# Two transformer blocks on one core: the order of the steps from an account of every engine, lent work tiles in the swiglu parts, and the keys' norm ahead of the scans

## The chip, the cores and the metric

One Trainium2 chip, one core of it. The time is the device time of one execution of the whole program in microseconds. Below, PE is TensorE, DVE is VectorE, ACT is ScalarE, POOL is GpSimd and SP is SyncE, whose queue carries the DMA transfers.

## What is computed

Two blocks in fp32 over 256 rows of width 1024. The first block has two layers, each with a swiglu, a mixing part (RWKV-7 beside a causal attention), cross-attention to a memory of 256 rows, and a second swiglu; a final norm ends it. The second block has an adaptive norm from a condition vector, an mLSTM beside a differential attention, and a hierarchical mixture of 32 experts. Cut to what bears on the change:

```python
def first_block(x, mem, rel_bias, ...):
    for l in range(DEPTH):
        x = x + FFN_RES_WEIGHT * swiglu_ffn(rms_norm(x, ffn1_norm_g[l]), ffn1_w_in[l], ffn1_w_out[l])
        proj = rms_norm(x, mix_norm_g[l]) @ w_mix_in[l]
        y_rwkv = rwkv7_time_mix(proj[..., :RWKV_PROJ], ...)
        y_moba = moba_attention(q_m, k_m, v_m, rel_bias)
        x = x + jnp.concatenate([y_rwkv, y_moba], axis=-1) @ w_mix_out[l]
        x = x + memory_cross_attention(...)
        x = x + FFN_RES_WEIGHT * swiglu_ffn(rms_norm(x, ffn2_norm_g[l]), ffn2_w_in[l], ffn2_w_out[l])
    return rms_norm(x, final_norm_g)

def rwkv7_time_mix(p, ...):
    ...
    decay = jnp.exp(-jnp.exp(w_log))
    a = jax.nn.sigmoid(a0 + a_lo @ a_up)
    kk = k * k_k
    kk = kk / jnp.maximum(jnp.sqrt(jnp.sum(kk * kk, axis=-1, keepdims=True)), 1e-12)
    b = kk * a
    # state = state * decay + (state @ -kk) b + v k, row after row
```

## The kernel before

**Weights.** All weights lie in one array of units; half a unit is a tile of 128 by 1024 floats, 512 KB, which SP loads into `raw` (four buffers, `RING`). Since products are exact to fp32 only in parts, each tile is split: ACT copies it to a rounded form `wh` (L369), DVE subtracts that to get the rest `wl` (L370), with two buffers of each in the first block. The activations have the same two parts, `XH` and `XL`. A product of 128 by 512 is then three matmuls, high by high, high by the weight's rest, and the rest by high (L398, L399, L400). A swiglu part takes 66 such tiles. A tile of a projection feeds 12 matmuls.

**Order.** Every part of the program is a generator. It issues some instructions and then yields two numbers: how long TensorE will be at work on them, and how many microseconds must pass until its next step should be issued. `Weave.step` (L260) keeps one clock `now`, adds the first number, and sets the task's due time by the second; of the tasks that are due it takes the one of the highest priority (the lowest number). All numbers are written by hand. The program thus sets the order of each engine's queue; every engine takes its queue in order, and waits on semaphores for data or for a buffer to come free.

```python
        if callable(r):
            t.need = r
        else:
            self.now += r[0]
            t.ready = self.now + r[1]
```

**PSUM.** Eight banks: four called `acc`, two `mm` for projections, two `tr` for transposes and small sums.

**Swiglu** (`ffn`, L625). Eleven chunks of 256 columns: a projection of gate and up into `mm`, tanh on ACT and two products on DVE, four transposes (L666) into `tr`, and the product with the next weights into the four `acc` banks. Behind the last chunk the four `acc` banks are finished one after the other, DVE adds each to x (L680), and `prep` (L518) makes the next part's input: for each half of x, transposes of two tiles of rows (L534), a scaling by DVE (L540), and the split by ACT and DVE (L542, L543). While it loads weights of the swiglu, the program also folds the tiles of the condition's projection into sums on DVE (`ada`, L1349).

**Mix** (`mix`, L685). Thirteen projections run as the main task at priority 10. Beside them run tasks for RWKV: `shifted` (L726) transposes and shifts a projection's result, `rwkv_early` (L774) prepares decay, keys and receptance for one of two groups of heads (a pair of 128-wide blocks each), `rwkv_chunk` (L986) solves two chunks of 128 rows by a chain of small matmuls and copies, and `rwkv_late` (L859) applies the state and norms the result. `moba` (L1159) does the attention, `xattn_k` the keys of the cross-attention.

In `rwkv_early` the order of the text is the order in each queue: two small matmuls per block (L790, L791), then on ACT per block a tanh, two exponentials (L794 to L796) and the square of the keys (L797), on DVE two scans (L804) and two products (L806, L807), and only then the norm of the keys. The squares are summed over each head by matmuls with a matrix of ones (L813), DVE takes a maximum (L815), POOL the power −1/2 over four columns (L816), ACT spreads the result over the heads (L818), once for each half of the rows, and PE transposes it (L825). The second and the third yield between them carry guessed delays of 0.6 and 1.5 us.

**Names.** In a row `tr<-csts,t1k` is a transpose or small sum into a `tr` bank, `mm<-wh,XH` a product of a projection, `acc<-wh,X` one of a swiglu's second product. `L398` and the like are lines of the kernel.

Of the kernel before, what the change touches and what calls it, by code (L numbers as in the profile page):

```python
# [19 lines left out]
P = 128  # L20
D = 1024
KT = 8
# [214 lines left out]
class Task:  # L237


    def __init__(self, gen, prio):  # L240
        self.gen, self.prio, self.ready, self.need, self.done, self.out = gen, prio, 0.0, None, False, None
# [4 lines left out]

class Weave:


    def __init__(self):  # L250
        self.now, self.tasks = 0.0, []
# [8 lines left out]
    def step(self, top=99):  # L260
        able = []
        for t in self.tasks:
            if t.prio > top:
                continue
            if t.need is not None:
                if not t.need():
                    continue
                t.need, t.ready = None, max(t.ready, self.now)
            able.append(t)
        t = next((t for t in able if t.ready <= self.now + 1e-6), None)  # L270
        if t is None:
            t = min(able, key=lambda z: z.ready)
            self.now = t.ready
        try:
# [4 lines left out]
            return  # L279
# [22 lines left out]
class Prog:  # L302
    def __init__(self, ctx, tc, a):
        self.tc, self.nc, self.a = tc, tc.nc, a
# [9 lines left out]
        self.weave = Weave()  # L314
# [5 lines left out]
        self.behind, self.stop = [], None  # L320

# [4 lines left out]
    def ps(self, tag):  # L326
        return self.pp.tile([P, 512], F32, name=self.nm(tag), tag=tag, bufs={"acc": 4, "mm": 2, "tr": 2}[tag])
# [7 lines left out]
    def k(self, tag, n, dt=F32):  # L335

        return self.kp.tile([P, n], dt, name=self.nm(tag), tag=tag, bufs=self.bufs[tag])

    def wtile(self, tag, dt):

        n = RING[tag]
        turn = self.turn.setdefault(tag, collections.deque())
        if not turn:
            turn.extend([self.wp] * n + [self.kp] * self.bufs.get(tag, 0))
            turn.extend([self.sp] * self.spare.get(tag, 0))
        pool = turn.popleft()
        bufs = {id(self.wp): n, id(self.kp): self.bufs.get(tag, 0), id(self.sp): self.spare.get(tag, 0)}[id(pool)]
        return pool.tile([P, 1024], dt, name=self.nm(tag), tag=tag, bufs=bufs)

    def lookahead(self, tag):  # L350

        return RING[tag] + self.spare.get(tag, 0) + self.bufs.get(tag, 0)

    def raw(self, name, j, i):
# [3 lines left out]
        else:  # L358
            src = self.a["w"][UNITS[name] + j, i]
        self.nc.sync.dma_start(t, src)  # L360
        return t


    def parts(self, raw):
        h, l = self.wtile("wh", F32R), self.wtile("wl", F32R)
        with ExitStack() as later:
            for z in self.behind:
                later.enter_context(self.tc.issue_after(z.ins))
            self.nc.scalar.activation(h, raw, AF.Copy)  # L369
            self.nc.vector.tensor_sub(l, raw, h.bitcast(F32))  # L370
        return h, l

    def weights(self, name, j, i):

        self.prefetch()
# [1848 lines left out]
```

## Time and profile before

| what | value |
|---|---|
| median of 3 runs | 2004.87 us |
| lowest and highest | 2003.45 us, 2007.29 us |
| the profiled execution | 2002.69 us |
| its span | 2000.9 us |
| its mean granted clock of TensorE | 0.988 |
| TensorE busy | 1915.2 us (96%) |
| VectorE busy | 1401.1 us (70%) |
| ScalarE busy | 1064.5 us (53%) |
| moved from HBM | 378.03 MB |

The span is that of the first to the last instruction; the time of the execution has 1.8 us more around it. A busy share tells how much of the span an engine spent in instructions. A stretch in which TensorE is granted half of its clock counts as busy too. A granted clock of 1.00 is 2.4 GHz, the lower level is 1.2 GHz. In a timeline the bracket behind a row gives how long the engine stood idle before it, and what ended the idle time.

### The profile page before, as it was taken

The numbers are of one execution on the slowest core, as the hardware profiler recorded it, in microseconds if no ns is written. First come the engines' busy times: TensorE is split into PE (matmuls) and PEld (weight loads), VectorE is DVE, ScalarE is ACT, GpSimd is POOL, SyncE is SP. The second block draws the span as 40 slices with busy tenths as digits, with TensorE's granted clock in tenths as the row PEclk, the third lists the DMA queues.
The fourth block names the chain that finished last, engine by engine and source line by source line (L and its number), as shares of the span: only waits on it lengthen the run. The fifth ranks groups of instructions, "written<-read, shape, count | busy, mean of one in ns | idle before, by whom it ended". The sixth has DMA issues, their size and how long they took to land.

```text
span 2000.9 us, 26350 instructions
## 1 busy us (share of the span) xinstructions
PE 1915.2 (96%) x9572; PEld 1540.8 (77%) x9572; DVE 1401.1 (70%) x2279; ACT 1064.5 (53%) x1608; POOL 70.4 (4%) x71
## 2 busy tenths in 40 slices
PE   8999989999999999999999999999989999999998
PEld 6788768778787878787777777787768777777776
DVE  6566686765566676666767654666687767999997
ACT  4444553555544454445545555444465556777675
POOL 0000011000000000000010000000010000000000
PEclk9999989999999999999999999999989998999999
DMA  6766431344366656665323253566654344999996
GB/s 218 251 227 215 154 124 55 102 127 169 119 218 219 208 193 212 221 210 180 133 81 106 69 180 116 197 209 213 216 180 146 128 158 141 322 344 357 327 345 235
DMA packets 114807, 381.42 MB, mean 191 GB/s; under 512 B 17080, under 2 KB 21864, under 8 KB 114544
## 3 DMA queue, kind: packets, MB, share of 16 engines
q1 hardware_dynamic: 114672, 379.68, 56.2%
q8 instruction: 77, 1.26, 0.3%
q14 instruction: 58, 0.48, 0.1%
HBM read 378.03 MB, written 3.17 MB: 191 GB/s over the span
## 4 chain that ended last, share of the span: by engine, by line
PE 69%; issue 12%; DVE 10%; ACT 4%; DMA 3%; POOL 1%; SPq 0%; DVEq 0%; POOLq 0%; ACTq 0%
PE mm L398 14%; PE mm L399 14%; PE mm L400 14%; DVE wl L370 5%; PE acc L400 4%; PE acc L398 4%; PE acc L399 4%; DMA raw<-in_w_dram 3%; ACT wh L369 3%; PE acc L1060 1%; PE acc L1291 1%; PE acc L1273 1%; PE acc L1195 1%; POOL rs L504 1%; PE tr L534 1%
## 5 line engine op out<-in xcount | busy, mean ns | idle before, releaser
L370 DVE TENSOR_TENSOR wl<-raw,wh 128x1024 fp32r<-128x1024 f32 x648 | 788.6, 1227 | 370.1 <-ACT wh L369 365.8
L369 ACT ACTIVATE wh<-raw 128x1024 fp32r<-128x1024 f32 x648 | 676.6, 1057 | 566.0 <-PE mm L400 381.1
L398 PE MATMUL mm<-wh,XH 128*128 128x512 f32 (+1 forms) x1744 | 695.2, 402 | 9.6 <-ACT s L733 3.6
L399 PE MATMUL mm<-wl,XH 128*128 128x512 f32 (+1 forms) x1744 | 690.8, 396 | 10.1 <-DVE wl L370 9.8
L400 PE MATMUL mm<-wh,XL 128*128 128x512 f32 (+1 forms) x1744 | 685.0, 394 | 1.4 <-DVE XL L543 1.1
L398 PEld LDWEIGHTS mm<-wh,XH 128*128 128x128 f32 x1744 | 330.8, 190 | 89.4 <-issue 12.7
L399 PEld LDWEIGHTS mm<-wl,XH 128*128 128x128 f32 x1744 | 330.7, 190 | 84.2 <-DVE wl L370 22.0
L400 PEld LDWEIGHTS mm<-wh,XL 128*128 128x128 f32 x1744 | 330.5, 190 | 68.8 <-DVE XL L543 3.1
L398 PE MATMUL acc<-wh,X 128*128 128x512 f32 x352 | 141.9, 409 | 2.1 <-ACT wh L369 2.1
L399 PE MATMUL acc<-wl,X 128*128 128x512 f32 x352 | 140.1, 398 | 0.4 <-DVE wl L370 0.4
L400 PE MATMUL acc<-wh,T 128*128 128x512 f32 x352 | 139.3, 396 | 0.0
L399 PEld LDWEIGHTS acc<-wl,X 128*128 128x128 f32 x352 | 66.9, 190 | 15.8 <-DVE wl L370 2.2
L398 PEld LDWEIGHTS acc<-wh,X 128*128 128x128 f32 x352 | 66.2, 189 | 16.6 <-ACT wh L369 3.1
L400 PEld LDWEIGHTS acc<-wh,T 128*128 128x128 f32 x352 | 66.7, 189 | 15.5
L1349 DVE SCALAR_TENSOR_TENSOR el<-raw,vecs,el 128x512 f32<-128x512 f32 x84 | 63.1, 752 | 21.1 <-DMA raw<-in_w_dram 18.7
L653 ACT ACTIVATE t1k<-mm,rh 128x256 f32<-128x256 f32 x88 | 41.8, 475 | 58.9 <-PE mm L400 58.9
L400 PE MATMUL acc<-wh,ah 128*128 128x512 f32 x128 | 50.0, 398 | 1.2 <-DVE ah L407 1.2
L399 PE MATMUL acc<-wl,ah 128*128 128x512 f32 x128 | 50.6, 398 | 0.0
L398 PE MATMUL acc<-wh,ah 128*128 128x512 f32 x128 | 45.6, 397 | 1.4 <-ACT ah L405 1.4
L657 DVE SCALAR_TENSOR_TENSOR t1k<-mm,rh,t1k 128x256 f32<-128x256 f32 x88 | 42.6, 484 | 3.0
L655 DVE SCALAR_TENSOR_TENSOR t1k<-t1k,mm 128x256 f32<-128x256 f32 x88 | 36.8, 418 | 9.0 <-ACT t1k L653 7.3
L556 POOL TENSOR_TENSOR rs<-s,emh 128x2 f32<-128x2 f32 x11 | 8.0, 729 | 945.3 <-DVE s L554 945.3
(480 smaller groups left out, 1888.1 us busy)
## 6 DMA issues: line engine op xcount, KB each, us to landing
raw<-in_w_dram SPq DMA_DIRECT2D x696, 512.0 KB
ext<-ext SPq DMA_DIRECT2D x1, 2048.0 KB
bi<-ext SPq DMA_DIRECT2D x8, 256.0 KB
K<-in_mem_dram SPq DMA_DIRECT2D x8, 256.0 KB
x<-in_x_dram SPq DMA_DIRECT2D x4, 256.0 KB
bi<-ext SPq DMA_DIRECT2D x8, 128.0 KB
w<-gates SPq DMA_DIRECT2D x2, 512.0 KB
out_dram<-x SPq DMA_DIRECT2D x4, 256.0 KB
```

The source lines that it names most:

```text
L369: self.nc.scalar.activation(h, raw, AF.Copy)
L370: self.nc.vector.tensor_sub(l, raw, h.bitcast(F32))
L398: mm(out, xh, wh, start=start, stop=False)
L399: mm(out, xh, wl, start=False, stop=False)
L400: mm(out, xl, wh, start=False, stop=stop)
L504: nc.gpsimd.tensor_tensor(r, ms, self.emh[:, :n], op=OP.pow)
L534: nc.tensor.transpose(tp[:, j * P:(j + 1) * P], xs[t][:, j * P:(j + 1) * P], self.ident)
L653: nc.scalar.activation(th, gu[t][:, :256], AF.Tanh, scale=rh[:, t:t + 1])
L655: nc.vector.scalar_tensor_tensor(tt, th, 1.0, gu[t][:, :256], op0=OP.add, op1=OP.mult)
L657: nc.vector.scalar_tensor_tensor(h, gu[t][:, 256:], r2h[:, t:t + 1], tt, op0=OP.mult, op1=OP.mult)
L1060: mm(zp[:, bs(j)], y[:, bs(j)], RH[:, j], start=True, stop=True)
L1349: self.nc.vector.scalar_tensor_tensor(self.mod, z, c, self.mod, op0=OP.mult, op1=OP.add)
```

## The change

**Order.** A class `Clock` keeps an account: for each engine the time at which it will be free, for each tile when its parts will be written and when it was last used, for each ring of buffers when the oldest comes free. `note` is called behind every instruction (a wrapper around the engines, line L378 in the trace afterwards) and adds a duration from a formula. A step now ends with `due(tiles)`, the time at which the account has these tiles written, or `room(ring)`, when a bank comes free; or with a small number against the end of the task's last work off TensorE. `now` follows the account's TensorE. Delays of 10 and more stay as they were. Some steps are cut finer: the two softmax halves go together in three phases, the norm after the time mix yields before each transpose, a projection yields before it takes banks and before each weight tile. `moba`'s priority goes from 4 to 1.5.

**Lent tiles.** In the swiglu parts the buffers of tags `sm`, `gr` and `pt`, which only other parts use, serve as one more `raw`, `wh` and `wl` (`raw` not in the last swiglu). At a swiglu's end the last tile but one is taken with a look-ahead of one.

**Keys' norm.** In `rwkv_early` the squares and the sums come first; one maximum and one power over eight columns serve both halves of the rows; the copies stand behind the tanh and the exponentials of both blocks. All other instructions are the same in kind and number: 4 fewer on DVE and 4 fewer on POOL.

```diff
+class Clock:
+    HOP, LAP = 0.06, dict(PE=0.0, DVE=0.08, ACT=0.1, POOL=0.0)
+    ...
+    def due(self, *aps):
+        t = 0.0
+        for z in aps:
+            name, runs, *_ = self.span(z)
+            for there, end, _ in self.wrote.get(name, ()):
+                if end > t and any(a < d and c < b for a, b in there for c, d in runs):
+                    t = end
+        return At(t + self.HOP)
+
+    def room(self, ring, n):
+        held = self.rings.get(ring, ())
+        return At(self.used.get(held[0], 0.0) + self.HOP if len(held) >= n else 0.0)
...
 class Weave:
...
-        else:
-            self.now += r[0]
-            t.ready = self.now + r[1]
+        elif r is not None:
+            if isinstance(r[1], At):
+                t.ready = max(self.now, r[1])
+            elif r[1] >= 10:
+                t.ready = self.now + r[1]
+            else:
+                t.ready = max(self.now, t.end + min(r[1], 0)) if r[1] else self.now
...
     def lookahead(self, tag):
-        return RING[tag] + self.spare.get(tag, 0) + self.bufs.get(tag, 0)
+        return RING[tag] + self.spare.get(tag, 0) + self.bufs.get(tag, 0) + len(self.loan.get(tag, ()))
...
     def proj(self, X, name, j, width=512, last=0):
+        yield 0, self.room("mm")
         out = [self.ps("mm") for _ in range(2)]
...
                 wh, wl = self.weights(name, j + u, i)
+                yield 0, self.due(wh)
...
-        w = [self.weights(name, 3 * NCH - 1, k) for k in range(2)]
+        w = [self.weights(name, 3 * NCH - 1, k, (99, 1)[k]) for k in range(2)]
...
-        C.append(self.spawn(self.moba(q, k, v, Y, [mq, mk]), 4))
+        C.append(self.spawn(self.moba(q, k, v, Y, [mq, mk]), 1.5))
...
     def rwkv_early(self, l, g, lo, rT, kT, need):
-        d, rd, sq = (self.k("el", 512) for _ in range(3))
+        sq, d, rd = (self.k("el", 512) for _ in range(3))
+        for b in range(2):
+            act(B(sq, b), B(kT, b), AF.Square, scale=vec("kk", b))
+        yield 0, self.due(sq)
+        s = self.ps("tr")
+        nr = []
+        for t in range(2):
+            for b in range(2):
+                mm(s[:, 4 * t + 2 * b:4 * t + 2 * b + 2], sq[:, b * S + t * P:b * S + (t + 1) * P], self.cst("bones"),
+                   start=True, stop=True)
+        n = self.k("s8", 8)
+        nc.vector.tensor_scalar_max(n, s[:, :8], 1e-24)
+        nc.gpsimd.tensor_tensor(n, n, self.emh[:, :8], op=OP.pow)
         zw, za = self.ps("tr"), self.ps("acc")
...
             act(B(rd, b), th, AF.Exp, bias=self.cdec[:, 1:2], scale=-DEC)
-            act(B(sq, b), B(kT, b), AF.Square, scale=vec("kk", b))
-        yield 1.0, 0
+        for t in range(2):
+            nr.append(self.k("t1k", 256))
+            nc.scalar.copy(nr[t].rearrange("p (h d) -> p h d", d=64), n[:, 4 * t:4 * t + 4, None].to_broadcast([P, 4, 64]))
+        yield 1.2, self.due(d, rd)
...
-        nr = []
-        for t in range(2):
-            s = self.ps("tr")
-            for b in range(2):
-                mm(s[:, 2 * b:2 * b + 2], sq[:, b * S + t * P:b * S + (t + 1) * P], self.cst("bones"), start=True, stop=True)
-            n = self.k("s8", 8)
-            nc.vector.tensor_scalar_max(n[:, :4], s[:, :4], 1e-24)
-            nc.gpsimd.tensor_tensor(n[:, :4], n[:, :4], self.emh[:, :4], op=OP.pow)
-            nr.append(self.k("t1k", 256))
-            nc.scalar.copy(nr[t].rearrange("p (h d) -> p h d", d=64), n[:, :4, None].to_broadcast([P, 4, 64]))
-        yield 0.1, 0.6
-        yield 0, 1.5
+        yield 0, self.due(*nr)
...
+LOAN = dict(raw=["sm"], wh=["gr"], wl=["pt"])
...
+                    p.lend({k: v for k, v in LOAN.items() if n < 7 or k != "raw"})
                     yield from p.ffn(f"ffn{part // 2 + 1}{l}", X)
+                    p.lend({})
```

On PE, at the keys' norm of the second pair of blocks in layer 0, before (`tr<-csts,el` are the sums of L813, `tr<-csts,t1k` the transposes of L825, `mm` the large products):

```order
L398 MATMUL mm_2351<-wh_2430,XH_1749 128x512
L399 MATMUL mm_2351<-wl_2431,XH_1749 128x512
L400 MATMUL mm_2351<-wh_2430,XL_1750 128x512
L813 MATMUL tr_2475<-csts,el_2442 128x2
L813 MATMUL tr_2483<-csts,el_2442 128x2
L813 MATMUL tr_2475<-csts,el_2442 128x2
L813 MATMUL tr_2483<-csts,el_2442 128x2
L825 MATMUL tr_2524<-csts,t1k_2481 128x128
L825 MATMUL tr_2552<-csts,t1k_2481 128x128
L825 MATMUL tr_2524<-csts,t1k_2489 128x128
L825 MATMUL tr_2552<-csts,t1k_2489 128x128
L398 MATMUL mm_2538<-wh_2499,XH_1749 128x512
```

The same place on PE in the changed kernel (`acc<-lora,waup` and `tr<-lora,waup` are the small matmuls of L791 and L790):

```order
L378 MATMUL mm_2363<-wh_2366,XL_1745 128x512
L378 MATMUL tr_2441<-csts,el_2436 128x2
L378 MATMUL acc_2450<-lora_1778,waup_1869 128x256
L378 MATMUL tr_2441<-csts,el_2436 128x2 x3
L378 MATMUL mm_2362<-wh_2414,XH_1744 128x512
L378 MATMUL mm_2362<-wl_2415,XH_1744 128x512
L378 MATMUL tr_2449<-lora_1778,waup_1869 128x256 x2
L378 MATMUL mm_2362<-wh_2414,XL_1745 128x512
```

Sums and transposes stood back to back; now 30 large products stand between them, 28 of them behind the last small matmul. For the first pair 10 stood between the first sums and the transposes, and 5 between the last sums and these; now 13 do.

On PE at the end of the first swiglu, before (`acc` are its last products, `tr<-csts,x` the transposes of L534; `x_72` and `x_73` are the two row tiles, each named once for either half of its columns):

```order
L398 MATMUL acc_106<-wh_1711,X_1687 128x512
L399 MATMUL acc_106<-wl_1712,X_1687 128x512
L400 MATMUL acc_106<-wh_1711,T_372_1688 128x512
L534 MATMUL tr_1752<-csts,x_72 128x128 x4
L534 MATMUL tr_1766<-csts,x_73 128x128 x4
L534 MATMUL tr_1797<-csts,x_72 128x128 x4
L534 MATMUL tr_1818<-csts,x_73 128x128 x4
L398 MATMUL mm_1764<-wh_1717,XH_1749 128x256
```

The same place in the changed kernel:

```order
L378 MATMUL acc_104<-wh_1701,T_376_1696 128x512
L378 MATMUL tr_1747<-csts,x_72 128x128 x4
L378 MATMUL tr_1756<-csts,x_73 128x128 x4
L378 MATMUL acc_106<-wh_1674,X_1695 128x512
L378 MATMUL acc_106<-wl_1675,X_1695 128x512
L378 MATMUL acc_106<-wh_1674,T_376_1696 128x512
L378 MATMUL acc_106<-wh_1701,X_1695 128x512
L378 MATMUL acc_106<-wl_1702,X_1695 128x512
L378 MATMUL acc_106<-wh_1701,T_376_1696 128x512
L378 MATMUL tr_1809<-csts,x_72 128x128 x3
L378 MATMUL mm_1779<-wh_1719,XH_1744 128x256
```

The first half's eight transposes moved ahead of the last six products; those of the second half now alternate with the first products of the next part.

On PE at the start of the first two chunks in layer 0, before (`tr<-csts,Y`, `acc<-X,A`, `acc<-Y,T` and `acc<-RH,Y` are steps of the chain of `rwkv_chunk`, once for each chunk):

```order
L1040 MATMUL tr_2624<-csts,Y_2233 128x128 x4
L398 MATMUL mm_2538<-wh_2590,XH_1749 128x512
L1040 MATMUL tr_2631<-csts,Y_2265 128x128 x4
L399 MATMUL mm_2538<-wl_2591,XH_1749 128x512
L400 MATMUL mm_2538<-wh_2590,XL_1750 128x512
L1046 MATMUL acc_2651<-X_2629,A_2234 128x128 x4
L1046 MATMUL acc_2659<-X_2636,A_2266 128x128 x4
L1053 MATMUL acc_2667<-Y_2233,T_609_2656 128x128 x4
L1053 MATMUL acc_2673<-Y_2265,T_611_2664 128x128 x4
L399 MATMUL mm_2539<-wl_2591,XH_1749 128x512
L400 MATMUL mm_2539<-wh_2590,XL_1750 128x512
```

The same place in the changed kernel:

```order
L378 MATMUL mm_2599<-wh_2602,XH_1744 128x512
L378 MATMUL tr_2546<-csts,Y_2211 128x128 x4
L378 MATMUL tr_2553<-csts,Y_2243 128x128 x4
L378 MATMUL acc_2566<-X_2551,A_2212 128x128 x4
L378 MATMUL acc_2574<-X_2558,A_2244 128x128 x4
L378 MATMUL acc_2582<-Y_2211,T_588_2571 128x128 x4
L378 MATMUL acc_2588<-Y_2243,T_590_2579 128x128 x4
L378 MATMUL tr_2622<-csts,s_593_2594 128x128
```

The projection's products between the steps are gone; eight transposes of the attention's queries and one large product follow, and then the next steps of the chain.

## Rows read from the trace of the kernel before

**Rows 1.** Page, part 1: busy us (share of the span) xinstructions

```profile
PE 1915.2 (96%) x9572; PEld 1540.8 (77%) x9572; DVE 1401.1 (70%) x2279; ACT 1064.5 (53%) x1608; POOL 70.4 (4%) x71
```

**Rows 2.** Windows by stage: from:to length, busy by engine, clock, DMA share, GB/s

```profile
core 0: us, PE busy (x) PEld busy (x) DVE busy (x) ACT busy (x) POOL busy (x), PEclk, DMA share, GB/s
212.60:451.00 238.40, 222.78 (x1431) 178.86 (x1430) 165.59 (x368) 128.99 (x256) 22.64 (x24) 0.98 0.34 108
...
734.10:930.70 196.60, 192.85 (x878) 156.80 (x876) 130.75 (x164) 89.37 (x112) 0.70 (x1) 1.00 0.63 209
...
1452.90:1676.00 223.10, 210.98 (x1044) 168.63 (x1045) 168.44 (x348) 124.31 (x199) 19.62 (x12) 0.98 0.50 167
```

**Rows 3.** Windows around the keys' norm, layer 0 twice and layer 1 twice

```profile
247.00:258.00 11.00, 7.84 (x30) 5.67 (x30) 8.69 (x22) 5.21 (x11) 3.79 (x4) 0.84 0.30 95
286.00:298.00 12.00, 7.76 (x26) 5.66 (x26) 11.51 (x35) 6.29 (x14) 5.08 (x4) 0.72 0.23 65
966.00:974.00 8.00, 4.83 (x16) 3.19 (x15) 7.82 (x16) 4.62 (x9) 2.24 (x3) 0.79 0.42 133
1004.00:1016.00 12.00, 8.01 (x30) 5.93 (x30) 11.05 (x35) 6.69 (x15) 5.35 (x4) 0.72 0.26 67
```

**Rows 4.** Timeline, first pair, layer 0: start, us, engine, line, operation [idle before]

```profile
249.78 0.41 ACT L818 COPY t1k<-s 128x256 f32<-128x256 f32 x1 [1.08 <-POOL s L816]
...
250.24 0.44 PE L825 MATMUL tr<-csts,t1k 128*128 128x128 f32 x2 [1.05 <-ACT t1k L818]
...
252.50 0.50 PE L398 MATMUL mm<-wh,XH 128*128 128x512 f32 x1 [1.82 <-ACT s L733]
```

**Rows 5.** Timeline, second pair, layer 0

```profile
286.77 0.50 ACT L796 ACTIVATE el<-t1k,cdec 128x256 f32<-128x256 f32 x1
...
288.76 0.14 DVE L815 TENSOR_SCALAR s<-tr 128x4 f32<-128x4 f32 x1
...
288.97 2.61 POOL L816 TENSOR_TENSOR s<-s,emh 128x4 f32<-128x4 f32 x2 [25.32 <-DVE s L815]
...
290.47 0.44 PE L825 MATMUL tr<-csts,t1k 128*128 128x128 f32 x2 [2.14 <-ACT t1k L818]
```

**Rows 6.** Timeline of POOL in the second block: a power over 8 columns

```profile
1530.35 1.67 POOL L504 TENSOR_TENSOR rs<-s,emh 128x8 f32<-128x8 f32 x1 [58.54 <-DVE s L502]
```

**Rows 7.** Timeline of PE in the first layer's second swiglu

```profile
606.22 0.39 PE L398 MATMUL mm<-wh,XH 128*128 128x512 f32 x1
...
606.45 0.39 PE L399 MATMUL mm<-wl,XH 128*128 128x512 f32 x1
```

**Rows 8.** Waits of PE in the first and last swiglu: us, times, longest

```profile
PE mm L399 <- DVE wl L370: 2.0, 3, 1.1
PE mm L399 <- DVE wl L370: 1.8, 4, 0.5
```

**Rows 9.** Page, part 5: xcount, busy, mean ns, idle before and releaser

```profile
L370 DVE TENSOR_TENSOR wl<-raw,wh 128x1024 fp32r<-128x1024 f32 x648 | 788.6, 1227 | 370.1 <-ACT wh L369 365.8
```

**Rows 10.** Timeline of SP near the start

```profile
48.83 0.60 SPq L485 DMA_DIRECT2D ext<-ext  x1
```

**Rows 11.** Windows near the start

```profile
58.00:62.00 4.00, 2.18 (x12) 1.58 (x10) 0.43 (x1) 0.87 (x1) 0.00 (x0) 1.00 0.92 364
62.00:66.00 4.00, 3.76 (x10) 2.95 (x11) 2.96 (x3) 1.62 (x3) 0.00 (x0) 0.57 0.46 161
```

**Rows 12.** Waits of PE over the whole span: us in total, times, longest

```profile
PE tr L534 <- DVE s L540: 4.9, 3, 1.6
...
PE tr L939 <- DVE YL L936: 2.6, 4, 0.8
...
PE tr L666 <- DVE t1k L657: 2.0, 3, 0.7
PE tr L1609 <- DVE E L1605: 1.9, 2, 1.2
```

**Rows 13.** Timeline of DVE at the end of the first swiglu

```profile
211.91 0.69 DVE L680 SCALAR_TENSOR_TENSOR x<-acc,x 128x512 f32<-128x512 f32 x1 [0.67 <-PE acc L400]
```

**Rows 14.** Windows: a chunk chain and attention in layer 0's mix

```profile
371.00:400.00 29.00, 28.99 (x273) 25.33 (x272) 16.16 (x30) 13.10 (x32) 1.19 (x2) 1.00 0.24 69
```

More of the change, by code (lines that the diff above doesn't have):

```diff
@@ new lines, with __init__, __getattr__, call @@
+class Timed:
+    def __init__(self, nc, clock):
+        self.nc = nc
+        for k, e in Clock.ENGINES.items():
+            setattr(self, k, TimedEngine(getattr(nc, k), e, clock))
+    def __getattr__(self, k):
+        return getattr(self.nc, k)
+class TimedEngine:
+    def __init__(self, eng, name, clock):
+        self.eng, self.name, self.clock = eng, name, clock
+    def __getattr__(self, op):
+        f = getattr(self.eng, op)
+        def call(*args, **kw):
+            r = f(*args, **kw)
+            self.clock.note(self.name, op, args, kw)
+            return r
+        return call
@@ L247, with __init__ @@
 class Weave:
-    def __init__(self):
-        self.now, self.tasks = 0.0, []
+    def __init__(self, clock):
+        self.now, self.tasks, self.clock = 0.0, [], clock
+        self.end = 0.0
     def add(self, gen, prio):
@@ L267, in step @@
                     continue
-                t.need, t.ready = None, max(t.ready, self.now)
+                t.need, t.ready, t.end = None, max(t.ready, self.now), max(t.end, self.end)
             able.append(t)
@@ L273, in step @@
             self.now = t.ready
+        self.clock.last = 0.0
         try:
@@ L278, in step @@
             self.tasks.remove(t)
-            return
+            r = None
+        t.end = self.end = max(t.end, self.clock.last)
+        self.now = max(self.now, self.clock.at["PE"])
         if callable(r):
             t.need = r
-        else:
-            self.now += r[0]
-            t.ready = self.now + r[1]
+        elif r is not None:
[3 more added lines that the diff above has]
+                t.ready = self.now + r[1]
+            else:
+                t.ready = max(self.now, t.end + min(r[1], 0)) if r[1] else self.now
     def finish(self, *tasks):
@@ L303, in __init__ @@
     def __init__(self, ctx, tc, a):
-        self.tc, self.nc, self.a = tc, tc.nc, a
+        self.clock = Clock()
+        self.tc, self.nc, self.a = tc, Timed(tc.nc, self.clock), a
         nc = self.nc
@@ L326, in ps, with room, due, tile @@
     def ps(self, tag):
[L327 removed]
+        n = BANKS[tag]
+        return self.tile(self.pp, [P, 512], F32, tag, tag, n)
+    def room(self, tag):
+        return self.clock.room((id(self.pp), tag), BANKS[tag])
+    def due(self, *aps):
+        return self.clock.due(*aps)
+    def tile(self, pool, shape, dt, nm, tag, n):
+        name = self.nm(nm)
+        self.clock.tile((id(pool), tag), n, name)
+        return pool.tile(shape, dt, name=name, tag=tag, bufs=n)
     @contextmanager
@@ L548, in prep @@
                     nc.scalar.activation(junk, xs[t], AF.Square, scale=D ** -0.5, accum_out=ss[:, 2 * hf + t:2 * hf + t + 1])
-            yield 0, 1.2
+                self.clock.quiet = False
+            half = slice(4 * hf, 4 * hf + 4)
+            yield 0, self.due(pair.H[:, half], pair.L[:, half])
             pair.ok[hf] = True
@@ L936, in rwkv_late @@
             tt(h4(yl), h4(yl), ss[t][:, :4, None].to_broadcast([P, 4, 64]), op=OP.mult)
+        for t in range(2):
+            yl = YL[t]
+            yield 0, self.due(yl)
             tp = self.ps("tr")
@@ L1175, in moba @@
                 nc.vector.tensor_tensor(cut[t](s), sp[:, :2 * n], cut[t](bi), op=OP.add)
-                yield 0.43 * (t + 1), 0.5
+                yield 0.43 * (t + 1), 0 if t == 0 else -0.5
             if i < 3:
                 bi = bias(*each[i + 1])
-            pv = [self.softmax(cut[t](s), cut[t](s), 2, (t + 1) * P) for t in range(2)]
-            yield 0, 4.5
+            pv = yield from self.softmax(*[(cut[t](s), cut[t](s), 2, (t + 1) * P) for t in range(2)])
             for t in range(2):
@@ L1274, in xattend @@
                                      KT[i][:, kb * S:(kb + 1) * S], start=kb == 0, stop=kb == 1)
+            sps.append(sp)
             yield 1.7, 0
-            pv.append(self.softmax(sm[:, t * 512:(t + 1) * 512], sp, 2, S))
-        yield 0, 3.5
+        pv = yield from self.softmax(*[(sm[:, t * 512:(t + 1) * 512], sps[t], 2, S) for t in range(2)])
         for i in range(2):
@@ L1318, in final_norm @@
             yield lambda: self.version[hf] >= use
-            yield 0, 0.9
+            yield 0, self.due(*[z[hf] for z in self.halves(self.x)])
             squares(0, hf)
```

254 lines of the change are left out of this document (176 added, 78 removed).

## The prediction

> **What bounds the kernel now.** I read the busy shares first, then the span cut into stages, then the stretches and the timeline around the longest stalls, then the list of TensorE's waits. The shares say that TensorE works 1915.2 of 2000.9 us, so 85.7 us are left in which it does nothing; VectorE is next with 1401.1 us [rows 1]. The time is TensorE's work plus its stalls, and the change leaves TensorE the same matmuls and transposes. So the question is only how many of the stalls go, and whether new ones come.
>
> The stages say where the stalls are [rows 2]: a swiglu part idles 196.60 − 192.85 = 3.8 us, a mix part 238.40 − 222.78 = 15.6 us, the stretch from the final norm through the second block's attention 12.1 us. The mix parts come first. Their granted clock of 0.98, against 1.00, points to a second loss, which busy time does not show: stretches in which TensorE counts as busy and runs at the lower of its two levels, 1.2 GHz.
>
> Inside a mix part both losses stand at the keys' norm [rows 3], once for each pair of head blocks. In layer 0 the first pair idles 11.00 − 7.84 = 3.2 us, and a mean clock of 0.84 over 11 us means 1.8 us of full speed lost; the second idles 4.2 and loses 12 × 0.28 = 3.4. The two places of layer 1 idle 3.2 and 4.0 us and lose 1.7 and 3.4. Together 14.6 us of idle and 10.3 us of clock, **24.9 us**.
>
> The timeline says why. The small power on GpSimd is followed by a copy on ScalarE for each half of the rows, and the transposes of L825 stand on TensorE's queue close behind. In the first pair they wait 1.05 us for the second copy, and the next product waits 1.82 us more for a copy that stood behind these on ScalarE [rows 4]. In the second pair nothing stands on TensorE between the sums of L813 and the transposes, which wait 2.14 us for the first of two powers that take 2.61 us together [rows 5].
>
> **The change part by part.**
>
> *Keys' norm first.* The squares and sums now precede the tanh, the exponentials and the scans, and one power over 8 columns takes the place of two over 4. Such a power took 1.67 us elsewhere [rows 6], against 2.61 for two [rows 5]. In the order, 13 large products now stand between sums and transposes for the first pair and 28 for the second. A large product starts 0.23 us after the one before [rows 7], so these cover 3.0 and 6.4 us. What has to fit is a maximum (0.14), the power (1.67) and two copies of 0.41: 2.6 us. For the second pair it is hidden whole. For the first it is not certain: ScalarE has six activations of 0.5 us, the tanh and exponentials, in its queue ahead of the copies [rows 5], so 3.0 + 0.8 = 3.8 us against 3.0. I leave 1 us there, with the clock staying up, and 1.3 us per layer for what ScalarE and VectorE do late: 4.6 us stay. Term **−20**; bounds −25 (all hidden) and −10 (the copies come late and the clock still falls once per layer).
>
> *Lent tiles.* The swiglu parts get a third pair of split tiles and a fifth raw tile from buffers that idle there. TensorE waits for the low half of a weight 13 times in the four parts, 6.7 us in all; the first part and the last are shown [rows 8]. Splitting a tile costs VectorE 1.23 us [rows 9], and its 12 products run 2.75 us [rows 7], so a split is late only when other VectorE work comes between. A third tile adds 2.75 us of cover to waits whose longest in these parts is 1.1 us. Term **−6**; bounds 0 (VectorE's own order is the cause) and −6.7.
>
> *Start of the program.* The 2 MB copy that spreads the bias table is issued at 48.83 us, among the weights [rows 10]. Later TensorE idles 1.8 and 0.2 us and runs 4 us at 0.57 [rows 11], 2.0 + 1.7 = 3.7 us. A fifth raw tile, and a copy issued three weight tiles earlier, cover a part: **−2**; bounds 0 and −3.7.
>
> *End of the swiglu.* The transposes of both halves of x stand together, and the later ones wait for VectorE to empty a bank: 4.9 us in three places [rows 12]. Now the first half goes ahead of the last six products (1.4 us), the second between products of the next part. What cannot be covered there is the last addition to x, 0.69 us [rows 13]. Term **−3.4**; bounds 0 and −4.9.
>
> *Guessed delays.* Of the waits behind a guess I count the three largest kinds that are left: the time mix's output transposes (2.6 us), the first chunk of a swiglu (2.0), the second block's weights E (1.9) [rows 12], 6.5 us. Where a chain is longer than the work at hand no order hides it, so I take two thirds, **−4.3**; bounds 0 and −6.5. Besides, a mix part idles 15.6 us [rows 2], of which 7.4 lie at the keys' norm in layer 0; of the other 8.2, in many short waits, I take a quarter, 2 us per layer: **−4**; bounds 0 and −16.
>
> *What it costs.* In the new order the first chunks' chain of the time mix has nearly no projection between its steps. With two pairs of blocks in two layers there are four such places, the later pair's with attention between. Two chunks alternate, each covering the other's copies. A stretch of 29 us of such chain and attention work, with little projection in it, was busy 28.99 us at clock 1.00 [rows 14]. So bare chains need not stall; but where VectorE has a weight to split in between (1.23 us, [rows 9]), a step is late. One per place: **+5**; bounds 0 and +20, four of them per place.
> A rule of the Trainium skill speaks against the change here ("TensorE: Matmul & The Clock Gate", section "A second HAM failure mode: psum-queue depth-cycling"): short idle times between groups of matmuls that cycle through PSUM banks let the clock go down and up, and the throughput suffers. By it this term would be near +50 instead of +5, as under the second rival. The stretch just named cycles through banks and does not bear it out.
>
> Sum: −20 − 6 − 2 − 3.4 − 4.3 − 4 + 5 = −34.7. The profiled execution took 2002.69 us; the median of three is 2004.87, 2.2 above. So 1968 us for such an execution and, 2.2 above it, **1970 us** for a median.
>
> **Rivals.** About 0.2%, 4 us, is what a measurement of this kernel can tell from no change.
>
> *The stalls move.* The account is a model of the chip that no trace corrects while it plans; ScalarE and VectorE take their work in order, so other instructions become late. Then what stays is what buffers and the shorter power bring: −6, −2 and half the keys' norm (−10), and the chains' +5: −13, 1992 us. For it: VectorE is busy 70% of the span [rows 1]. Against it: the largest waits stand where a whole chain was issued without any cover, and there the order changes most.
>
> *The bare chains drop the clock (slower).* If each of the four places, some 29 us long, ran at the 0.57 that those 4 us at the start had [rows 11], it would lose 29 × 0.43 = 12.5 us: +50 in place of +5. With the gains of 39.7 that is +10, 2015 us. It decides from 39.7 / 4 = 9.9 us lost in each place. For it: the clock fell after each of the idle times at the keys' norm [rows 3]. Against it: it stayed at 1.00 through such a chain [rows 14]. The skill's rule named above would give this time.
>
> *More is hidden.* If the 12 us that I leave of the mix parts' short waits go too, and half of the 12.1 us idle in the second block's attention: 1970 − 18 = 1952 us.
>
> *It orders little.* The norm's gain is lost again on the first pair's late copies and on chain steps at their upper bounds: −10 − 6 + 20, and the small terms at 0, is +4, within the 4 us of before: 2001 to 2009.
>
> **How the numbers follow.** Forecast, 1958 to 1983: 0.57. The stalls move, 1983 to 2000: 0.18. More is hidden, 1943 to 1958: 0.12. Little: 0.05. Slower: 0.08. The slower end, the unchanged case and the lower half of the best one are left out of the range, 0.19 in all, and the upper edge is drawn in a little, since the second case centres on 1992: **1951 to 1997**. Faster by over 0.2%: 0.87; the same 0.05; slower 0.08.
>
> **What would show it.** Right: at the keys' norm of either layer no idle of TensorE much over 1 us and no half clock behind it; fewer than five waits for a low half in the four swiglu parts; no wait over 1 us for the normalised x at a swiglu's end; mix parts some 12 us shorter, swiglu parts 2 to 4. Wrong: new waits of TensorE inside the chunk chains, with the clock falling behind them; or the norm's transposes still waiting for the copies, with the tanh and exponentials ahead of these.

## The result and the profile after

The changed kernel takes 1979.93 us, median of 4 runs (1978.89 to 1985.92), against 2004.16 us before; the ratio is 0.9884, with a 95% interval of 0.9860 to 0.9908. That is 24 us less where 34 were forecast, inside the range. The profiled execution took 1985.92 us, the slowest of the four and 16.8 us less than the profiled one before, so its stages show less gain than the median. Its mean granted clock is 0.987; the other three had 0.990 and 0.991.

In the profile after, nearly every instruction has line L378, that of the wrapper, and is told apart by its tiles. Part 1 of the page, to be held against [rows 1]:

```profile
PE 1913.3 (96%) x9572; PEld 1551.5 (78%) x9572; DVE 1398.0 (70%) x2275; ACT 1062.2 (54%) x1608; POOL 72.7 (4%) x67
```

The span is 1984.1 us, so 1984.1 − 1913.3 = 70.8 us of TensorE's idle time are left of 85.7: 14.9 of the 16.8 us are idle time. The windows by stage, as in [rows 2]:

```profile
208.40:440.90 232.50, 220.10 (x1424) 180.66 (x1425) 163.31 (x365) 127.00 (x252) 24.67 (x22) 0.99 0.34 108
725.40:920.00 194.60, 193.12 (x878) 157.50 (x878) 129.19 (x163) 90.12 (x116) 0.69 (x1) 1.00 0.63 206
1435.40:1660.00 224.60, 210.28 (x1050) 169.71 (x1050) 168.63 (x349) 125.81 (x203) 18.55 (x12) 0.98 0.50 166
```

The swiglu part idles 1.5 us (3.8 before), the mix part 12.4 (15.6 before), the second block 14.3 (12.1 before). At the keys' norm, first and second pair of layer 0, then of layer 1, as in [rows 3]:

```profile
232.00:247.00 15.00, 13.63 (x78) 10.73 (x76) 12.40 (x29) 11.56 (x23) 2.94 (x2) 1.00 0.30 102
280.00:292.00 12.00, 8.83 (x39) 6.60 (x38) 10.12 (x26) 7.86 (x16) 1.27 (x2) 0.72 0.25 71
...
945.00:960.00 15.00, 13.50 (x77) 10.60 (x77) 12.83 (x28) 10.54 (x21) 3.90 (x2) 1.00 0.24 81
994.00:1008.00 14.00, 10.99 (x45) 8.79 (x44) 11.10 (x27) 8.19 (x16) 1.26 (x2) 0.63 0.20 59
```

The first pairs idle 1.4 and 1.5 us at full clock: of 9.9 us lost there before (idle 3.2 and 3.2, clock 1.8 and 1.7), 2.9 are left. (A wait some 7 us behind these windows has grown; it is shown with the bare chains below.) The second pairs idle 3.2 and 3.0 us, and lose 12 × 0.28 = 3.4 and 14 × 0.37 = 5.2 us of clock: 14.8 us, against 15.0 before. There the change gained next to nothing in this execution; a second profile, shown with the changed kernel's rerun below, has 13.6 us. The timeline of the second pair in layer 0 shows why, first ScalarE, then VectorE, then TensorE:

```profile
276.96 1.06 ACT L378 ACTIVATE wh<-raw 128x1024 fp32r<-128x1024 f32 x1 [4.61 <-PE mm L378]
...
279.62 1.70 ACT L378 ACTIVATE el<-t1k,cdec 128x256 f32<-128x256 f32 x4
281.22 0.70 ACT L378 COPY t1k<-s 128x256 f32<-128x256 f32 x2
...
282.54 0.70 ACT L378 ACTIVATE s<-mm,rh 128x512 f32<-128x512 f32 x1
```

```profile
283.92 1.23 DVE L378 TENSOR_TENSOR_SCAN el<-el,start 128x512 f32<-128x512 f32 x1
...
287.45 0.87 DVE L378 SCALAR_TENSOR_TENSOR el<-K,vecs,tr 128x256 f32<-128x256 f32 x2
```

```profile
281.67 0.74 PE L378 MATMUL tr<-csts,t1k 128*128 128x128 f32 x4 [0.67 <-ACT t1k L378]
283.29 0.50 PE L378 MATMUL mm<-wh,XH 128*128 128x512 f32 x1 [0.88 <-ACT s L378]
...
287.98 1.97 PE L378 MATMUL tr<-csts,Y 128*128 128x128 f32 x8 [1.63 <-DVE el L378]
```

The power on GpSimd starts at 273.05, takes 1.64 us and is done at 274.7, but ScalarE stands idle for 4.61 us before a weight's split, whose tile TensorE still holds. The tanh, the exponentials and the norm's copies are behind it in the queue, so the copies start only at 281.22, and the transposes (0.67 us) and the next product (0.88 us) wait. A third wait is new: the transposes put their results into both `tr` banks, and VectorE reads them only at 287.45, behind the scans; until then the chunk chain's next transposes have no bank (1.63 us). The row names VectorE's `el`, the reader of these banks, and not the `Y` they transpose.

### The profile page after: what moved, and what is told of

The parts are those of the page before. It is cut to its first block, busy times and chain, and to the rows that moved or that the text cites. A ratio compares the mean times of both kernels' runs of the same rounds, so it can differ in the third digit from the quotient of the medians.

```text
span 1984.1 us, 26329 instructions
## 1 busy us (share of the span) xinstructions
PE 1913.3 (96%) x9572; PEld 1551.5 (78%) x9572; DVE 1398.0 (70%) x2275; ACT 1062.2 (54%) x1608; POOL 72.7 (4%) x67
## 4 chain that ended last, share of the span: by engine, by line
PE 72%; issue 12%; DVE 10%; ACT 3%; DMA 2%; POOL 1%; SPq 0%; DVEq 0%; POOLq 0%; ACTq 0%
PE mm L378 45%; PE acc L378 22%; PE tr L378 5%; DVE wl L378 4%; ACT wh L378 2%; DVE s L378 1%; DVE el L378 1%; DMA raw<-in_w_dram 1%; POOL rs L378 1%; DMA K<-in_mem_dram 1%; DVE XL L378 1%; DVE x L378 1%; DVE AR L378 0%; DVE t1k L378 0%; ACT s L378 0%
## 5 line engine op out<-in xcount | busy, mean ns | idle before, releaser
L378 DVE TENSOR_TENSOR wl<-raw,wh 128x1024 fp32r<-128x1024 f32 x648 | 786.3, 1225 | 370.6 <-ACT wh L378 368.8
L378 ACT ACTIVATE wh<-raw 128x1024 fp32r<-128x1024 f32 x648 | 676.1, 1057 | 538.8 <-PE mm L378 368.5
L378 PE MATMUL mm<-wh,XH 128*128 128x512 f32 (+1 forms) x1744 | 698.2, 402 | 10.9 <-ACT s L378 3.3
L378 PE MATMUL mm<-wl,XH 128*128 128x512 f32 (+1 forms) x1744 | 687.4, 394 | 3.8 <-DVE wl L378 3.5
L378 PE MATMUL mm<-wh,XL 128*128 128x512 f32 (+1 forms) x1744 | 685.6, 393 | 2.7 <-DVE XL L378 2.7
L378 PEld LDWEIGHTS mm<-wh,XH 128*128 128x128 f32 x1744 | 330.3, 190 | 84.7 <-issue 8.1
L378 PEld LDWEIGHTS mm<-wl,XH 128*128 128x128 f32 x1744 | 330.1, 189 | 78.5 <-DVE wl L378 13.3
L378 PEld LDWEIGHTS mm<-wh,XL 128*128 128x128 f32 x1744 | 329.6, 189 | 74.7 <-DVE XL L378 4.0
L378 PE MATMUL acc<-wh,X 128*128 128x512 f32 x352 | 143.0, 406 | 0.0
L378 PE MATMUL acc<-wl,X 128*128 128x512 f32 x352 | 139.0, 395 | 0.0
L378 PE MATMUL acc<-wh,T 128*128 128x512 f32 x352 | 138.8, 394 | 0.0
L378 PE MATMUL acc<-wh,ah 128*128 128x512 f32 x256 | 85.9, 398 | 2.9 <-ACT ah L378 1.5
L378 DVE SCALAR_TENSOR_TENSOR el<-raw,vecs,el 128x512 f32<-128x512 f32 x84 | 63.1, 751 | 34.1 <-DMA raw<-in_w_dram 32.6
L378 PEld LDWEIGHTS acc<-wh,T 128*128 128x128 f32 x352 | 66.3, 188 | 16.1
L378 PEld LDWEIGHTS acc<-wl,X 128*128 128x128 f32 x352 | 66.4, 189 | 13.8
L378 PEld LDWEIGHTS acc<-wh,X 128*128 128x128 f32 x352 | 66.2, 188 | 13.6
L378 POOL TENSOR_TENSOR rs<-s,emh 128x2 f32<-128x2 f32 (+2 forms) x28 | 30.7, 1100 | 1195.1 <-DVE s L378 1187.8
L378 ACT ACTIVATE t1k<-mm,rh 128x256 f32<-128x256 f32 x88 | 41.8, 474 | 53.0 <-PE mm L378 52.6
L378 PEld LDWEIGHTS acc<-wh,ah 128*128 128x128 f32 x256 | 47.9, 188 | 15.6 <-DVE ah L378 2.3
L378 DVE SCALAR_TENSOR_TENSOR t1k<-t1k,mm 128x256 f32<-128x256 f32 x120 | 50.1, 418 | 8.7 <-ACT t1k L378 4.7
L378 PE MATMUL acc<-wl,ah 128*128 128x512 f32 x128 | 50.5, 398 | 0.1
L378 PEld LDWEIGHTS tr<-csts,t1k 128*128 128x128 f32 (+1 forms) x262 | 32.9, 141 | 19.9 <-PE mm L378 3.2
```

The lines of the kernel that those rows point to most:

```text
L378: r = f(*args, **kw)
```

## The experiments

Differences are of medians. They ran in three groups, each beside a kernel before of its own: without the lent tiles, only these, only the norm moved, and the norm behind the scans beside 2003.19 us; the account's order alone, tiles and norm, the attention's priority in the changed kernel, and the memory's rows beside 2003.44; the rest beside 2003.60.

**Without the lent tiles.**

```diff
-LOAN = dict(raw=["sm"], wh=["gr"], wl=["pt"])
+LOAN = {}
-        w = [self.weights(name, 3 * NCH - 1, k, (99, 1)[k]) for k in range(2)]
+        w = [self.weights(name, 3 * NCH - 1, k) for k in range(2)]
```

> The changed kernel without the lent tiles (and without the limit on look-ahead that came with them). If the lent tiles pay by themselves, as the terms of 6 and 2 us say and as the changed trace seems to show (the start and the swiglu parts lost some 10 us of stalls), TensorE waits again for low halves in the swiglu parts and the time is 1986 to 1991 us. If the account's order has already hidden those waits, it stays at 1978 to 1983 us.

1993.09 us, ratio to before 0.9958 (0.9943 to 0.9974). The tiles are worth 12.5 us in the changed kernel (1980.56 in its own rerun, below), more than expected.

**Only the lent tiles, in the kernel before.** The edit is `lend`, the lent buffers and the limit on look-ahead, put into the kernel before.

> The kernel before with only the lent tiles (and their limit on look-ahead). If a third pair of split tiles covers waits whatever the order, 1994 to 1998 us, against 2004 before. If those waits come from the order of VectorE's queue, 2002 to 2006 us.

1990.21 us, ratio 0.9939 (0.9927 to 0.9952): 13.0 us, more than expected and, in this order, more than any other part. Its waits of TensorE, against [rows 12] and, for the low half, against the first line here, which is of the kernel before:

```profile
PE mm L399 <- DVE wl L370: 9.8, 17, 1.4
```

```profile
PE mm L407 <- DVE wl L378: 4.3, 5, 1.4
...
PE tr L542 <- DVE s L548: 1.5, 3, 0.5
```

The waits for the low half of a weight fell from 9.8 to 4.3 us (one is left in the four swiglu parts), and those at a swiglu's end from 4.9 to 1.5. The stretch that lost 3.7 us near the start [rows 11] has no stall left:

```profile
50.00:75.00 25.00, 25.00 (x112) 20.43 (x111) 15.77 (x21) 11.71 (x14) 0.00 (x0) 1.00 0.89 303
```

5.5 + 3.4 + 3.7 = 12.6 us, near the gain, though small waits elsewhere have grown (those of a swiglu's first transposes by 1.5 us). All idle time of TensorE fell from 85.7 to 75.6 us. So the swiglu's end, which the prediction had given to the new order, is served by the tiles and their limit alone; which of these two does it was not tried apart.

**Without the fifth raw tile.**

```diff
-LOAN = dict(raw=["sm"], wh=["gr"], wl=["pt"])
+LOAN = dict(wh=["gr"], wl=["pt"])
```

> The changed kernel with the split tiles lent but not the fifth raw tile. If the 13 us of the lent tiles are nearly all the third pair of split tiles, 1979 to 1984 us. If the start of the program and the swiglu parts wait for loads, as the stall of 3.7 us near 60 us had it, 1984 to 1992 us.

1979.73 us, ratio 0.9875 (0.9860 to 0.9890): the same as with it. In this order the gain is the split tiles' (with the limit on look-ahead, which stays), at the start of the program too, where TensorE has no stall without the fifth tile either:

```profile
50.00:75.00 25.00, 25.00 (x113) 20.46 (x112) 17.98 (x23) 12.19 (x15) 0.00 (x0) 1.00 0.74 260
```

**Only the keys' norm moved, in the kernel before.**

```diff
+        for b in range(2):
+            act(B(sq, b), B(kT, b), AF.Square, scale=vec("kk", b))
+        yield 0, 1.2
...
-        yield 1.0, 0
+        yield 1.2, 0
...
-        yield 0.1, 0.6
         yield 0, 1.5
```

> The kernel before with only the keys' norm moved ahead of the scans and done in one power, with guessed delays of 1.2 and 1.5 us. If the move itself frees TensorE, its idle time at the four places falls from 14.6 us to under 5 us and the time is 1988 to 1996 us. If a guess is not enough and the copies stand behind tanh and exponentials on ScalarE, 1999 to 2005 us.

1996.47 us, ratio 0.9973 (0.9962 to 0.9985), between the two: 6.7 us. The runs spread from 1990.78 to 2001.89, and the profiled one is the fastest. The transposes of the first pair in layer 0 no longer wait; the product behind them does, for a bank that ScalarE empties behind its other work:

```profile
250.73 0.50 PE L398 MATMUL mm<-wh,XH 128*128 128x512 f32 x1 [3.27 <-ACT s L733]
```

At the norm no idle time went. At the four places TensorE idles 3.3, 4.0, 3.3 and 4.0 us, 14.6 as before, and 83.9 us in the whole span, against 85.7. What went is the half clock behind these places, 10.3 us before [rows 3] and none in this execution. The two places of layer 0:

```profile
246.00:257.00 11.00, 7.74 (x40) 6.22 (x39) 10.90 (x28) 6.30 (x12) 2.62 (x3) 1.00 0.21 68
284.00:300.00 16.00, 12.04 (x63) 8.68 (x62) 14.43 (x38) 10.03 (x19) 3.06 (x2) 1.00 0.31 99
```

The median of the twelve runs' mean clocks is 0.992, against 0.988 before; 0.4% of 2000 us is 8 us, an estimate near the 6.7. Why the clock holds better here is not shown.

**The norm behind the scans again, in the changed kernel.** The edit puts the old piece back, with `self.due(*nr)` before its transposes.

> The changed kernel with the keys' norm behind the scans again, in two halves with two powers, its transposes due when the account has the copies. If the move itself carries most of the gain in the mix parts, the waits for the powers and copies come back and the time is 1990 to 1996 us. If the account, by putting large products between sums and transposes, hides the norm wherever it stands, the time stays at 1978 to 1984 us.

1999.68 us, ratio 0.9986 (0.9975 to 0.9996): in the account's order the move is worth 19 us, more than expected. Most of it lies elsewhere than at the norm. With the norm late, the second pair of heads ends last in its mix part and bare, as TensorE's timeline shows in layer 0:

```profile
420.65 0.58 PE L378 MATMUL tr<-csts,YL 128*128 128x128 f32 x2 [4.58 <-DVE s L378]
422.34 0.66 PE L378 MATMUL tr<-csts,YL 128*128 128x128 f32 x2 [1.11 <-DVE YL L378]
424.29 0.79 PE L378 MATMUL mm<-wh,XH 128*128 128x512 f32 x1 [1.29 <-ACT XH L378]
```

These are 7.0 us, and 6.9 in layer 1. At the norm itself TensorE waits 7.7 us for the copies, no more than the 9.1 us that it idles at the four places in the changed kernel.

**The account's order alone.** Both edits together: no tiles lent, the norm in its old place.

> The changed kernel with neither the lent tiles nor the moved norm: the account's order alone. If the parts add up as the runs without one of them did (13 us for the tiles, 20 for the norm in this order), 2010 to 2016 us, slower than before by some 10 us, so that the account by itself costs time. If the order by itself removes waits that were guessed too short, as its term of 12 us in the prediction had it, 1990 to 1998 us.

2006.76 us, ratio 1.0018 (1.0008 to 1.0028): slower than before by 3.3 us, though not by the 10 that adding up gave. The same three waits end its mix parts in both layers (4.6 us the longest), and TensorE idles 92.7 us in all, 7.0 more than before.

**Tiles and norm, in the guessed order.** Both edits in the kernel before.

> The kernel before, in its guessed order, with the lent tiles and the moved norm. If the two add (13 and 7 us) and the account is worth little, 1981 to 1986 us, within 4 us of the changed kernel. If the account carries part of the gain, 1987 to 1993 us.

1985.43 us, ratio 0.9913 (0.9898 to 0.9927). The account (with the attention's priority) is worth 4.9 us on top of it, at the edge of the noise.

**The attention's priority.** In the changed kernel it goes back to 4 (the edit below); in the kernel with tiles and norm in the guessed order it goes to 1.5 (the same edit reversed).

```diff
-        C.append(self.spawn(self.moba(q, k, v, Y, [mq, mk]), 1.5))
+        C.append(self.spawn(self.moba(q, k, v, Y, [mq, mk]), 4))
```

> The changed kernel with the attention's priority at 4 again in place of 1.5. If attention between the steps of the second chunk chains only crowds ScalarE and VectorE there, 1974 to 1978 us. If it is what fills these chains, it comes late, stands bare at the end of the mix parts, and the time is 1984 to 1995 us.

2001.03 us, ratio 0.9983 (0.9970 to 0.9995): 20.5 us slower, more than expected. From 370 us to the end of layer 0's mix TensorE idles 5.2 us at a clock of 0.96, and 1.1 us at full clock in the changed kernel:

```profile
370.00:446.00 76.00, 70.78 (x429) 55.64 (x425) 39.61 (x79) 38.45 (x85) 2.01 (x2) 0.96 0.31 102
```

```profile
370.00:441.00 71.00, 69.94 (x462) 56.84 (x459) 40.34 (x81) 39.72 (x88) 3.20 (x4) 1.00 0.35 111
```

> The kernel before, in its guessed order, with the lent tiles, the moved norm and the attention's priority of 1.5: all of the change but the account. If the account's share (5 us between the kernel with tiles and norm and the changed one) is only this priority, 1978 to 1982 us. If the priority pays only where the account has emptied the chunk chains (21 us there), 1984 to 1995 us here.

1989.12 us, ratio 0.9929 (0.9915 to 0.9942): 3.7 us slower than with priority 4, though the intervals overlap: no gain, at any rate. The priority pays only in the account's order, and the account only with the priority: at priority 4 the account makes the kernel with tiles and norm 15.6 us slower (1985.43 to 2001.03).

**Transposes of the memory's rows due with their load.**

```diff
                 xs = [x(t, hf) for t in range(2)]
+                yield 0, self.due(*xs)
```

> The changed kernel with one more step: the transposes of the memory's rows are due when the account has their load landed, where they now follow its issue at once. TensorE waits 2.7 and 1.4 us for these loads in the changed trace. If that wait stands on the path, 1974 to 1978 us; if the time is only moved to the end of the mix part, where the same tasks end, 1978 to 1982 us.

1982.54 us, ratio 0.9893 (0.9879 to 0.9908): no gain. TensorE's waits for these loads were 3.7 us in the changed kernel's first profile (2.5 and 1.2) and are 1.0 here, the first line. But the changed kernel's second profile, the second line, has 1.1 without the edit:

```profile
PE tr L378 <- DMA K<-in_mem_dram: 1.0, 2, 0.6
```

```profile
PE tr L378 <- DMA K<-in_mem_dram: 1.1, 2, 0.5
```

So the fall can't be put down to the edit: the wait differs by 2.6 us between two executions of one kernel. TensorE's whole idle time is 70.8, 70.4 and, with the edit, 71.0 us, so other waits make up for this one; a stall that can be seen need not be on the path.

**The copies first, for the second pair.**

```diff
+        def spread():
+            ...
+        if g == 1:
+            spread()
         zw, za = self.ps("tr"), self.ps("acc")
...
-        for t in range(2):
-            nr.append(self.k("t1k", 256))
-            nc.scalar.copy(...)
+        if g == 0:
+            spread()
```

> The changed kernel with the two copies of the norm ahead of tanh and exponentials on ScalarE for the second pair of blocks. If TensorE's waits of 0.8 and 1.1 us there, and the clock that falls behind them, come from these copies' place in ScalarE's queue, 1970 to 1976 us. If the scans, which then start 0.8 us later, hold up the chunk chain's masks on VectorE instead, 1979 to 1986 us.

1985.66 us, ratio 0.9915 (0.9901 to 0.9928): 5 us slower; my theory of the copies' place fell, and where the 5 us lie was not found. TensorE's waits from 270 to 290 us:

```profile
PE mm L378 <- ACT s L378: 2.1, 1, 2.1
PE tr L378 <- DVE el L378: 1.7, 2, 1.4
```

The transposes no longer wait, but the product behind them now does for the whole 2.1 us, and the bank's wait is still there, split in two (1.40 and 0.34). The banks are held longer, not shorter: the norm's transposes now fill them from 279.64 us on, where it was 281.67, and VectorE reads them at 287.39 and 288.38, still behind its scans, which start 0.7 and 1.1 us later than in the changed kernel. The time is that of the second branch; whether by its cause is not shown.

**The changed kernel again.**

> The changed kernel once more, unchanged, beside the other three on one chip. 1978 to 1983 us, as its four runs had it. If the clock's stretches at half speed are the same in every execution, its profile shows those of the first one (25 us of full speed lost, 8.5 of them at the second pair of the keys' norm in either layer); if they vary, a faster execution shows some of these places at full clock with the same waits.

1980.56 us (1977.30 to 1985.79), ratio 0.9881 (0.9866 to 0.9896). Its profile is again of a long execution, 1985.79 us, so no faster one shows what it does better. But the stretches at half speed do vary. From 239 to 258 us, the first line from the first profile and the second from this one, the idle time is the same, and only this one loses clock, 1.7 us:

```profile
239.00:258.00 19.00, 16.01 (x102) 12.54 (x101) 18.20 (x44) 10.37 (x20) 5.18 (x3) 1.00 0.28 88
```

```profile
239.00:258.00 19.00, 15.96 (x93) 12.42 (x92) 16.71 (x38) 8.87 (x17) 5.18 (x3) 0.91 0.26 86
...
994.00:1008.00 14.00, 10.76 (x60) 8.90 (x60) 12.66 (x29) 7.84 (x16) 1.26 (x2) 0.76 0.17 51
```

At the second pair of layer 1 it is the other way round, 0.76 here and 0.63 in the first profile.

## Why the prediction was right, and where its steps were not

| | guessed order | account's order |
|---|---|---|
| neither tiles nor norm | 2003.4 | 2006.8 |
| lent tiles | 1990.2 | 1999.7 |
| norm moved | 1996.5 | 1993.1 |
| both | 1985.4 | 1980.6 |

The account's order has the attention's priority of 1.5 with it. The next table has TensorE's idle time in the profiled execution (us, from part 1 of each page) and, behind it, the median of the mean granted clocks of all executions:

| | guessed order | account's order |
|---|---|---|
| neither tiles nor norm | 85.7, 0.988 | 92.7, 0.985 |
| lent tiles | 75.6, 0.9885 | 83.7, 0.985 |
| norm moved | 83.9, 0.992 | 79.0, 0.990 |
| both | 75.0, 0.992 | 70.8, 0.990 |

The tiles take away 8.2 to 10.1 us of idle time in each of the four pairs. The norm's move raises the clock in either order; idle time it takes away only in the account's, 13 to 14 us. The account adds 7 to 8 us of idle time with the norm late and takes 4 to 5 away with the norm moved.

*Sign and range* held, and TensorE's stalls were the right thing to count: 14.9 of the 16.8 us between the two profiled executions are idle time. The sum was 10 us too good. That it came so near is in part luck, as the terms show. The tiles' 12.5 us and the 7.2 found at the norm's places below make some 20 of the 24; the rest is not placed.

*Lent tiles, start, swiglu's end* (−6, −2, −3.4): together −11.4, and −13.0 was measured in the kernel before (7.1 to 13.0 over the four pairs of the first table). The total stands, its division does not: the fifth raw tile brings nothing (−2 forecast for it and the earlier copy), and the end of the swiglu went with the tiles.

*Keys' norm* (−20) is the step that failed. At its four places the loss fell from 24.9 to 17.7 us, 7.2 in place of 20; alone, the move brought 6.7 us, and that from the clock. That the changed kernel without it is 19 us slower, near the 20, is a coincidence: 14 of these us stand at the end of the mix parts. The prediction called the second pair "hidden whole", by counting products against power and copies, and doubted the first. It was the other way round: the first pairs went from 9.9 to 2.9 us, the second stayed at 14.8. The count left out two things: ScalarE's queue, where the copies stand behind a split that waits for TensorE's tile, and the two `tr` banks, which the earlier transposes now hold through the scans. This is read from the timeline; the one edit that moved the copies up did not bring the time back. That a wait for a bank took the place of a wait for data was under none of the rivals by name; it is what "the stalls move" would look like.

*Guessed delays* (−8.3) and *chains* (+5), net −3.3: the account alone costs 3.3 us, and brings 4.9 once tiles and norm are there. The three kinds of waits that I counted, 6.5 us, are 6.6 in the changed kernel (output transposes 2.0, first chunks 2.0, weights E 2.6), so this −4.3 brought nothing. The reason for the rest is not at the waits I listed, but at the end of the mix parts, which the order makes sensitive to which task is last: 19 us for the norm's place, 20.5 for the attention's priority.

*The bare chains* (+5). The second rival's +50 did not come, but its mechanism did, in small. In the second pair's chain of layer 0, right behind that pair's stall, TensorE is busy without a gap; the 1.0 us of idle time in the next window are output transposes of the time mix, which waited 0.85 and 0.73 us there before, and the 0.96 is the end of the stretch at half speed that began at 284 us:

```profile
289.00:312.00 23.00, 23.00 (x228) 20.92 (x227) 16.25 (x40) 7.99 (x15) 4.10 (x5) 0.96 0.18 59
312.00:341.00 29.00, 27.98 (x187) 22.38 (x187) 23.06 (x64) 12.68 (x23) 3.91 (x2) 1.00 0.24 72
```

In the first pair's chain a wait has grown, from 0.4 us (the first line, before) to 1.5 (the second) in either layer. VectorE splits a weight first and writes `rkv` behind it, which is the late step that the term was for:

```profile
265.28 0.30 PE L1021 MATMUL tr<-csts,rkv 128*128 128x128 f32 x1 [0.38 <-DVE rkv L748]
```

```profile
253.67 0.30 PE L378 MATMUL tr<-csts,rkv 128*128 128x128 f32 x1 [1.47 <-DVE rkv L378]
```

```profile
251.60 1.53 DVE L378 TENSOR_TENSOR wl<-raw,wh 128x1024 fp32r<-128x1024 f32 x1
253.05 0.86 DVE L378 SCALAR_TENSOR_TENSOR rkv<-tr,omu,sh 128x256 f32<-128x256 f32 x2
```

That is 1.1 us more, near the 1.25 us per place of the forecast. Behind it the clock fell, in layer 1 in both profiles of the changed kernel and in layer 0 in the second one. Layer 1, in the first:

```profile
960.00:972.00 12.00, 10.49 (x59) 8.37 (x58) 9.71 (x24) 4.93 (x10) 2.85 (x3) 0.86 0.42 134
```

This costs 12 × 0.14 = 1.7 us, not 12.5. The Trainium skill's rule of short idle times between groups ("TensorE: Matmul & The Clock Gate", section "A second HAM failure mode: psum-queue depth-cycling") agrees with these traces in kind, since the clock fell behind idle times of 1.5 us here and of 0.67 and 0.88 us at the second pair; where the chain had no idle time, the clock did not fall anew.

*The signs.* Three waits for a low half are left in the four swiglu parts, and a swiglu part is 2.0 us shorter, as named; one wait for the normalised x is 1.1 us long, just over the 1 us named. The mix part of layer 0 is 5.9 us shorter, not 12. Both signs of being wrong are there: the second pair's transposes still wait for copies with the exponentials ahead of them, and the first pair's chain has a new wait with the clock falling behind it.

No version beat the changed kernel clearly; the one without the fifth raw tile equals it.

## What to carry to other kernels

When a step is moved ahead, list what its results occupy until their reader comes, banks as well as buffers, and what stands ahead of each of its instructions in the in-order queues; a count of covering work alone calls hidden what is only late elsewhere. A third buffer in a ring whose filler is now and then late is cheap to estimate from the waits, and came out much as estimated in either order. Read idle time and granted clock apart, and over several executions: the norm's move left TensorE's idle time as it was in the guessed order, and its gain there is one of the clock. Before calling a wait gone through an edit, look for it in a second profile of the kernel without the edit. Parts of a change should be tried alone in both orders: here the new order costs time by itself and pays, a little, only with the norm moved and the attention's priority changed.

## What the runs showed of the hardware that was not expected

The clock's stretches at half speed are not fixed by the waits. I had expected them behind idle times of some 3 us. Only the norm moved, and norm with tiles, have the same wait for the same product in layer 0, 3.27 and 3.26 us. With the norm alone, 11 us around it are shown above (246 to 257 us, clock 1.00). With tiles as well:

```profile
241.00:252.00 11.00, 7.74 (x31) 6.02 (x30) 9.52 (x26) 6.01 (x12) 2.02 (x3) 0.84 0.26 91
```

Equal busy time, but 1.8 us of full speed lost in one of them. The two profiles of the changed kernel differ in the same way, as shown with its rerun. The changed kernel's four first executions had a mean clock of 0.987, 0.991, 0.990 and 0.991 at 1985.92, 1978.89, 1980.67 and 1979.20 us. Why an execution is granted more or less stays open.
